# One-row tile first, and the first store set beside the third load: a row-gradient kernel that lives on its DMA queues

## The chip, the core and the metric

The kernel runs on one core of a Trainium2 chip. The metric is the device time of one execution in microseconds (us), taken as the median of several runs. Three executions of the kernel before took 1245.61, 1249.69 and 1249.73 us; the median is 1249.69 us.

## The reference

```python
def setup_inputs():
    return {"x": np.random.randn(8192, 8192).astype(np.float32)}

def reference(x):
    return np.gradient(x, axis=1)
```

Along each row of 8192 numbers, every inner element of the output is half the difference of its right and left neighbours. The first element is x[1] - x[0], the last x[8191] - x[8190]. Input and output are 268.44 MB each.

## The kernel before, in words

**Tiles.** The 8192 rows are cut into 21 groups of 384 rows and a rest of 128 rows. In a group each of the 128 partitions holds three whole rows one behind the other (`G = 3`), 24576 numbers. A group is loaded as two tiles of `W` = 12288 columns. The first tile of a group stores its first `CUT` = 12224 columns; the second stores the remaining 12352, for which it needs 64 columns from the end of the first (and one more to their left). The rest of 128 rows is one tile more, with one row of 8192 columns to a partition, and it comes last. That makes 43 tiles, numbered 0 to 42: 42 loads of 6144 KB and one of 4096 KB, 21 stores of 6112 KB, 21 of 6176 KB and one of 4096 KB.

**Slots.** Four buffers (`NB = 4`) take turns: tile i lives in slot i mod 4. A result is written into the same slot, 64 columns further left (`SH`), so load and store of a tile use one buffer. Load i+4 therefore has to wait until store i has landed.

**Queues.** All loads are issued by SyncE (SP, line 60) on one hardware DMA queue (q1 in the profile), all stores by ScalarE (ACT, line 127) on another (q10). Both queues are served by the same 16 DMA engines. A transfer has 128 partition rows, eight for each engine. The order in which instructions are issued is the order in which they are written (`manual_schedule`), and waits that a kept one implies are declared away in `chain`.

**Work on a tile.** When load i has landed, GpSimd (POOL) takes the one-sided differences at row ends and row starts into the small tile `ends` (line 83, two instructions). For the second tile of a group it also copies 65 columns from the slot of the first (line 90, the "halo"). VectorE (DVE) then runs one custom instruction over the tile (line 101, the difference times one half) and puts the saved row ends and starts in place with two small copies (line 124). Then ACT issues the store. For tile 0 alone there is an extra VectorE instruction (line 111): it reads 800 columns of the slot, writes them to a tile `spare` that nobody uses, and so holds the first store back.

The lines that set the order of the loads:

```python
        needed = [stores[i - NB]] if i >= NB else []        # L61
        ...
        for i in range(NB):                                  # four loads at the start
            load(i)
        ...
                if i - 1 + NB < nt:                          # behind a halo copy
                    load(i - 1 + NB)
        ...
            if (first or i == nt - 1) and i + NB < nt:       # behind a second tile's store
                load(i + NB)
```

Of the kernel before, what the change touches and what calls it, by code (L numbers as in the profile page):

```python
# [1 line left out]

# [4 lines left out]


@with_exitstack
def kernel(  # L10
    ctx: ExitStack,
    tc: tile.TileContext,
    x: bass.AP,
    out: bass.AP,
):
    nc = tc.nc
    P = nc.NUM_PARTITIONS
    n, m = x.shape
    NB = 4
    G = 3  # L20
    SH = 64
    IN = 2 * SH
    W = G * m // 2
    CUT = W - SH
    f32 = x.dtype

    tiles = []
    ngroups = n // (P * G)
    left = n - ngroups * P * G
    for g in range(ngroups):  # L30
        rows = slice(g * P * G, (g + 1) * P * G)
        xr = x[rows, :].rearrange("(p q) m -> p (q m)", p=P)
        orr = out[rows, :].rearrange("(p q) m -> p (q m)", p=P)
        tiles.append((xr[:, 0:W], orr[:, 0:CUT], 0, W, CUT))
        tiles.append((xr[:, W : 2 * W], orr[:, CUT : 2 * W], W, W, 2 * W))
    for r in range(n - left, n, P):
        tiles.append((x[r : r + P, :], out[r : r + P, :], 0, m, m))
    nt = len(tiles)

    pool = ctx.enter_context(tc.tile_pool(name="pool", bufs=1))  # L40
    pad = pool.tile([P, 32], f32, name="pad", tag="pad")
    slots = [pool.tile([P, IN + W], f32, name=f"slot{k}", tag=f"slot{k}") for k in range(NB)]
    ends = pool.tile([P, nt, 4], f32, name="ends", tag="ends")
    spare = pool.tile([P, 800], f32, name="spare", tag="spare")
    loads, stores, halos = [], [], {}
    in_front = {}

    def chain(i, ins, *needed):
        group, engine = f"slot{i % NB}", ins.ins.engine
        keep = [o.ins for o in needed]  # L50
        if in_front.get(engine, (None,))[0] == group:
            keep.append(in_front[engine][1])
        tc.declare_no_dep(ins.ins, group=group, keep=keep, reason="implied by the needed step")
        tc.add_to_no_dep_group(group, ins.ins)
        in_front[engine] = group, ins.ins
        return ins

    def load(i):
        src, _, _, w, _ = tiles[i]
        ins = nc.sync.dma_start(out=slots[i % NB][:, IN : IN + w], in_=src)  # L60
        needed = [stores[i - NB]] if i >= NB else []  # L61
        if i - NB + 1 in halos:
            needed.append(halos[i - NB + 1])
        loads.append(chain(i, ins, *needed))

    with tc.manual_schedule():
        for i in range(NB):
            load(i)
        for i in range(nt):
            b = slots[i % NB]  # L70
            _, dst, first, w, last = tiles[i]
            begin = CUT if first else 0
            at = lambda c: IN + c - first
            row = [c for c in range(0, G * m, m) if begin <= c < last]
            tail = [c for c in range(m - 1, G * m, m) if begin <= c < last]

            pieces = [(tail, -1, 0, 2), (row, 0, 1, 0)]
            taken = []
            for cols, lo, hi, e in pieces:
                k = len(cols)  # L80
                a = at(cols[0])
                z = a + (k - 1) * m + 1
                ins = nc.gpsimd.tensor_sub(  # L83
                    out=ends[:, i, e : e + k],
                    in0=b[:, a + hi : z + hi : m],
                    in1=b[:, a + lo : z + lo : m],
                )
                taken.append(chain(i, ins, loads[i]))
            if first:
                ins = nc.gpsimd.tensor_copy(  # L90
                    out=b[:, IN - SH - 1 : IN],
                    in_=slots[(i - 1) % NB][:, IN + W - SH - 1 : IN + W],
                )
                tc.declare_no_dep(ins.ins, group=f"slot{(i - 1) % NB}", keep=[], reason="implied by the subtractions in front")
                halos[i] = chain(i, ins, *taken)
                taken.append(halos[i])
                if i - 1 + NB < nt:
                    load(i - 1 + NB)
            a = at(begin) + (0 if first else 1)
            z = at(last) - (1 if last % m == 0 else 0)  # L100
            ins = nc.vector._custom_dve(  # L101
                dve_ops.TENSOR_TENSOR_REDUCE_SUB_MAX,
                out=b[:, a - SH : z - SH],
                in0=b[:, a + 1 : z + 1],
                in1=b[:, a - 1 : z - 1],
                s0=0.0,
                s1=0.5,
            )
            done = chain(i, ins, *taken)
            if i == 0:  # L110
                ins = nc.vector._custom_dve(  # L111
                    dve_ops.TENSOR_TENSOR_REDUCE_SUB_MAX,
                    out=spare[:, :],
                    in0=b[:, IN + W - 800 : IN + W],
                    in1=b[:, IN + W - 800 : IN + W],
                    s0=0.0,
                    s1=0.5,
                )
                done = chain(i, ins, done)
            for cols, lo, hi, e in pieces:  # L120
                k = len(cols)
                a = at(cols[0]) - SH
                z = a + (k - 1) * m + 1
                ins = nc.vector.tensor_copy(out=b[:, a:z:m], in_=ends[:, i, e : e + k])  # L124
                done = chain(i, ins, done)
            a = at(begin) - SH
            ins = nc.scalar.dma_start(out=dst, in_=b[:, a : a + last - begin])
            stores.append(chain(i, ins, done))
            if (first or i == nt - 1) and i + NB < nt:
                load(i + NB)  # L130


# [1 line left out]
_INS = ['x']  # L134
_OUTS = [((8192, 8192), 'float32')]


# [23 lines left out]
```

## Time and profile before

| | |
|---|---|
| median of 3 runs | 1249.69 us (1245.61 to 1249.73) |
| profiled execution | 1250.2 us, its span 1248.4 us |
| VectorE busy | 563.6 us, 45% of the span |
| GpSimd busy | 18.4 us, 1% |
| moved | 536.91 MB, mean 430 GB/s over the span |
| load of 6144 KB, issue to landing | median 50.8 us |
| store of 6176 KB / 6112 KB, issue to landing | median 51.4 / 51.6 us |

The span is the stretch that the profiler's records cover; the execution's own time is 1.8 us longer. The profile's table of 40 slices gives, for each fortieth of the span, the mean busy share of the 16 DMA engines (9 is 90% or more) and the GB/s that they moved. A packet is counted in the slice in which it starts. One data packet is one partition's row of a transfer, 48 KB for most loads.

### The profile page before, as it was taken

The numbers are of one execution on the slowest core, as the hardware profiler recorded it, in microseconds if no ns is written. First come the engines' busy times: TensorE is split into PE (matmuls) and PEld (weight loads), VectorE is DVE, ScalarE is ACT, GpSimd is POOL, SyncE is SP. The second block draws the span as 40 slices with busy tenths as digits, with TensorE's granted clock in tenths as the row PEclk, the third lists the DMA queues.
The fourth block names the chain that finished last, engine by engine and source line by source line (L and its number), as shares of the span: only waits on it lengthen the run. The fifth ranks groups of instructions, "written<-read, shape, count | busy, mean of one in ns | idle before, by whom it ended". The sixth has DMA issues, their size and how long they took to land.

```text
span 1248.4 us, 450 instructions
## 1 busy us (share of the span) xinstructions
DVE 563.6 (45%) x130; POOL 18.4 (1%) x111
## 2 busy tenths in 40 slices
DVE  4544444444444444444454444444444545444442
POOL 0000000000000000000000000000000000000000
DMA  9999999999999999999999999999999999999997
GB/s 403 426 429 427 439 442 430 428 429 447 433 429 428 434 443 431 429 429 442 438 430 429 431 442 435 430 429 442 436 432 429 431 440 436 432 427 438 438 431 329
DMA packets 12388, 536.91 MB, mean 430 GB/s; under 512 B 1376, under 2 KB 1376, under 8 KB 1376
## 3 DMA queue, kind: packets, MB, share of 16 engines
q1 hardware_dynamic: 6192, 268.44, 49.9%
q10 hardware_dynamic: 6192, 268.44, 49.7%
q14 instruction: 4, 0.03, 0.0%
HBM read 268.44 MB, written 268.44 MB: 430 GB/s over the span
## 4 chain that ended last, share of the span: by engine, by line
another core or an unknown queue 92%; DMA 3%; issue 2%; POOL 1%; DVE 1%; SPq 0%; POOLq 0%; DVEq 0%
DMA slot<-in_x_dram 3%; POOL ends L83 1%; DVE slot L101 1%; POOL slot L90 0%; SPq L60 0%; POOLq L156 0%; DVE slot L124 0%; DVEq L156 0%
## 5 line engine op out<-in xcount | busy, mean ns | idle before, releaser
L101 DVE CUSTOM_DVE_ANT_0 slot<-slot 128x12223 f32<-128x12223 f32 (+2 forms) x43 | 552.9, 12859 | 663.9 <-POOL ends L83 340.8
L83 POOL TENSOR_TENSOR ends<-slot 128x1 f32<-128x1 f32 (+1 forms) x86 | 14.5, 193 | 1201.4 <-DMA slot<-in_x_dram 1201.4
L124 DVE COPY slot<-ends 128x1 f32<-128x1 f32 (+1 forms) x86 | 9.7, 157 | 1.4
L90 POOL COPY slot<-slot 128x65 f32<-128x65 f32 x21 | 5.0, 238 | 0.0
L111 DVE CUSTOM_DVE_ANT_0 spare<-slot 128x800 f32<-128x800 f32 x1 | 1.0, 992 | 0.0
L145 POOL MEMSET const-float32-0.0<- 128x1 f32 x1 | 0.1, 98 | 0.2 <-issue 0.2
L145 POOL MEMSET const-bfloat16-1.0<- 128x1 bf16 x1 | 0.1, 101 | 0.0
L145 POOL MEMSET const-uint8-127<- 128x1 uint8 x1 | 0.1, 101 | 0.0
L145 POOL MEMSET const-float32-1.0<- 128x1 f32 x1 | 0.1, 98 | 0.0
## 6 DMA issues: line engine op xcount, KB each, us to landing
slot<-in_x_dram SPq DMA_DIRECT2D x42, 6144.0 KB, 50.8
out_dram<-slot ACTq DMA_DIRECT2D x21, 6176.0 KB, 51.4
out_dram<-slot ACTq DMA_DIRECT2D x21, 6112.0 KB, 51.6
slot<-in_x_dram SPq DMA_DIRECT2D x1, 4096.0 KB, 45.9
out_dram<-slot ACTq DMA_DIRECT2D x1, 4096.0 KB, 18.4
```

What stands on the lines that cost most here:

```text
L83: ins = nc.gpsimd.tensor_sub(out=ends[:, i, e : e + k], in0=b[:, a + hi : z + hi : m], in1=b[:, a + lo : z + lo : m],)
L90: ins = nc.gpsimd.tensor_copy(out=b[:, IN - SH - 1 : IN], in_=slots[(i - 1) % NB][:, IN + W - SH - 1 : IN + W],)
L101: ins = nc.vector._custom_dve(dve_ops.TENSOR_TENSOR_REDUCE_SUB_MAX, out=b[:, a - SH : z - SH], in0=b[:, a + 1 : z + 1], in1=b[:, a - 1 : z ...
L111: ins = nc.vector._custom_dve(dve_ops.TENSOR_TENSOR_REDUCE_SUB_MAX, out=spare[:, :], in0=b[:, IN + W - 800 : IN + W], in1=b[:, IN + W - 80 ...
L124: ins = nc.vector.tensor_copy(out=b[:, a:z:m], in_=ends[:, i, e : e + k])
L145: nc = _bacc.Bacc("TRN2", target_bir_lowering=False, num_devices=1)
```

## The change

The rest of 128 rows becomes tile 0 instead of tile 42, and the groups follow as tiles 1 to 42, starting at row 128. The extra VectorE instruction of tile 0 covers 1400 columns instead of 800, from the slot's start. The last tile is now the second half of a group; its VectorE work is cut at a row's start (column 16384) into two pieces of 4160 and 8192 output columns, each followed by its own small copies and its own store. The condition that decides where a load is issued in the program follows the new numbering.

```diff
+    SPARE = 1400
...
-    ngroups = n // (P * G)
-    left = n - ngroups * P * G
-    for g in range(ngroups):
-        rows = slice(g * P * G, (g + 1) * P * G)
+    left = n % (P * G)
+    for r in range(0, left, P):
+        tiles.append((x[r : r + P, :], out[r : r + P, :], 0, m, m))
+    singles = len(tiles)
+    for r in range(left, n, P * G):
+        rows = slice(r, r + P * G)
...
-    for r in range(n - left, n, P):
-        tiles.append((x[r : r + P, :], out[r : r + P, :], 0, m, m))
...
-    spare = pool.tile([P, 800], f32, name="spare", tag="spare")
+    spare = pool.tile([P, SPARE], f32, name="spare", tag="spare")
...
-            a = at(begin) + (0 if first else 1)
-            z = at(last) - (1 if last % m == 0 else 0)
...
+            cuts = [begin, last]
+            if i == nt - 1:
+                cuts[1:1] = [c for c in row if c > begin]
+            done = None
+            for lo, hi in zip(cuts, cuts[1:]):
+                a = at(lo) + (1 if lo % m == 0 else 0)
+                z = at(hi) - (1 if hi % m == 0 else 0)
                 ins = nc.vector._custom_dve(
                     dve_ops.TENSOR_TENSOR_REDUCE_SUB_MAX,
-                    out=spare[:, :],
-                    in0=b[:, IN + W - 800 : IN + W],
-                    in1=b[:, IN + W - 800 : IN + W],
+                    out=b[:, a - SH : z - SH],
+                    in0=b[:, a + 1 : z + 1],
+                    in1=b[:, a - 1 : z - 1],
...
+                done = chain(i, ins, *taken, *([done] if done else []))
+                if i == 0:
+                    ins = nc.vector._custom_dve(
+                        dve_ops.TENSOR_TENSOR_REDUCE_SUB_MAX,
+                        out=spare[:, :],
+                        in0=b[:, IN : IN + SPARE],
+                        in1=b[:, IN : IN + SPARE],
...
+                for cols, e in ((tail, 2), (row, 0)):
+                    inside = [k for k, c in enumerate(cols) if lo <= c < hi]
+                    if inside:
...
+                        ins = nc.vector.tensor_copy(out=b[:, a:z:m], in_=ends[:, i, e : e + k])
+                        done = chain(i, ins, done)
+                a = at(lo) - SH
+                ins = nc.scalar.dma_start(out=dst[:, lo - begin : hi - begin], in_=b[:, a : a + hi - lo])
+                stored = chain(i, ins, done)
+            stores.append(stored)
-            if (first or i == nt - 1) and i + NB < nt:
+            if (first or i < singles) and i + NB < nt:
                 load(i + NB)
```

## The prediction

> **What bounds the kernel now.** I read the page's parts 1 to 3 first: is any engine full?
>
> ```profile
> DVE 563.6 (45%) x130; POOL 18.4 (1%) x111
> DMA  9999999999999999999999999999999999999997
> GB/s 403 426 429 427 439 442 430 428 429 447 433 429 428 434 443 431 429 429 442 438 430 429 431 442 435 430 429 442 436 432 429 431 440 436 432 427 438 438 431 329
> q1 hardware_dynamic: 6192, 268.44, 49.9%
> q10 hardware_dynamic: 6192, 268.44, 49.7%
> ```
>
> The DMA engines are full in every slice but the last, half by loads (q1), half by stores (q10). VectorE is idle more than half the time. The windows view puts numbers on the stages (columns: stretch and its length, DVE and POOL busy, clock, DMA share, GB/s):
>
> ```profile
> 100.00:600.00 500.00, 226.85 (x54) 7.14 (x42) 1.00 1.00 433
> 600.00:1200.00 600.00, 267.63 (x61) 9.01 (x53) 1.00 1.00 434
> 1236.00:1242.00 6.00, 0.00 (x0) 0.00 (x0) 1.00 0.84 360
> 1242.00:1248.40 6.40, 0.00 (x0) 0.00 (x0) 1.00 0.05 20
> ```
>
> At 433.5 GB/s the 536.9 MB take 1238.5 us, so only about 10 of the span's 1248.4 us can be anything but bytes. Where are they? The DMA view of 28 to 48 us, in slices of 0.5 us, shows packets starting together on all engines:
>
> ```profile
> GB/s 492 98 0 1376 98 98 492 983 98 0 1278 197 98 0 1475 0 98 0 0 0 1369 98 98 295 1180 0 98 1271 196 0 196 1376 0 98 782 685 0 98 1376 98
> ```
>
> The crests stand 3 or 4 slices apart, one packet (48 KB at 433.5/16 GB/s = 1.81 us), but between 35.0 and 38.0 us there are 6: the load packet ahead of the first store's took 3.0 us, 1.2 more, on all engines. The same view of 1242 us to the end, in slices of 0.16 us:
>
> ```profile
> DMA  0400000004000000400000004000000000000000
> GB/s 0 205 0 0 0 0 0 0 0 205 0 0 0 0 0 0 205 0 0 0 0 0 0 0 205 0 0 0 0 0 0 0 0 0 0 0 0 0 0 0
> ```
>
> Four lone packets, 1.2 us apart (32 KB each): one DMA engine still works and fifteen are done. In the trace's landing records the last store lands on the first engine at 1241.35 us, on the fifteenth at 1243.24, on the last at 1247.47: this engine is 4.2 us behind. Following its 688 packets back, each to the one that ended where it began, I find it 1.2 us long at the first load packet, 1.6 at the first store, and then 4.75 us in 27 stretched packets, nearly all loads beside a boundary between two stores (0.34 at 90 us, 0.85 at 148, 0.73 at 389) and rare after 560 us, when it trails the others. The 10 us are: 1.7 to the first packet, 0.7 in it, 1.2 at the first store, 4.2 of the last engine, about 1.3 behind its last packet, and under 1 unassigned.
>
> **The change, part by part.**
>
> *Tile order.* The same 43 loads and 43 tiles, the same bytes: 0. Packets cost their bytes: 48 KB took 1.815 us and 32 KB 1.213 us.
>
> *The first store's place.* These rows give the times:
>
> ```profile
> 18.68 12.89 DVE L101 CUSTOM_DVE_ANT_0 slot<-slot 128x12223 f32<-128x12223 f32 x1 [18.68 <-POOL ends L83]
> 31.61 0.99 DVE L111 CUSTOM_DVE_ANT_0 spare<-slot 128x800 f32<-128x800 f32 x1
> 32.77 70.41 ACTq L127 DMA_DIRECT2D out_dram<-slot  x4
> 1220.05 8.69 DVE L101 CUSTOM_DVE_ANT_0 slot<-slot 128x8190 f32<-128x8190 f32 x1 [10.69 <-POOL ends L83]
> ```
>
> 8190 against 12223 elements give 1.042 ns per element and 0.16 us fixed (800 would be 0.99, as measured); 1400 make 1.62 us. Load 0 is 8 x 0.602 = 4.8 us shorter, so VectorE starts at 13.9, ends its pass at 22.6, the extra one at 24.2, the copies at 24.4, where ACT issues store 0. Before, the issue came 1.35 us after load 2's first packet (31.42), and load packets two and three went ahead of the store. Now, 4.8 us earlier than in the packet records of before (29.6 and 31.4), load 1's eighth packet starts at 24.8 and load 2's first at 26.6; issued 0.36 us ahead of the eighth (0.46 before), the store follows load 2's first packet, at about 29.6. So packet k of store j runs beside packet k of load j+2. The extra 0.63 us of VectorE costs nothing: loads 1 to 3 keep the engines full until 81. Without that cover it would cost 0.63. The 1.2 us at a first store I leave in: nothing here takes it away (bounds 0 and -1.2).
>
> *Slots.* Load 4 waits for store 0, which lands at about 53.7 us, and its turn comes when load 3 ends, at 81: 27 us ahead (22 before: issued at 66.9, first packet at 88.8). Load 5 and the rest stand behind it in SP's queue, with their own stores to wait for, and the halo copies they need are over 50 us old. No starving: 0. Median issue to landing should rise for loads from 50.8 to about 57, and fall for stores from 51.5 to about 44 (13.6 us after landing they are issued, and two periods of 29 us after it they end).
>
> *The last tile.* One VectorE pass becomes two (4159 elements, 4.49 us; 8190, 8.69 us) with a third copy (0.15 us), and one store becomes two. Count from T, where the last engine ends its final load packet. One more store packet (1.8) and the landing (0.4) precede POOL and VectorE (0.6); the first piece is issued at T+7.5, the second at T+16.5. That engine has store packets until T+16.3 (1.8 + 8 x 1.81) and, with the first piece (8 x 0.614), until T+21.2. From issue to first packet it took 1.0 us at the first load and 5.3 at the first store, which queued behind three packets; by the worse the second piece is 0.6 late, by the better 3.7 early. I take 0, by the row of an empty queue. The engines that are ahead may stand still 2 to 4 us; they are not last. The 128 more packets are 8 on each engine: 1.213 and 1.815 us leave 9 ns fixed in a packet, so 0.07 us.
>
> *The boundaries.* Now both queues change tile at once on every engine, 41 times. Before, each change has the other queue's data beside it. Rows near it: load 0 to load 1 alone, no gap; store 40 to store 41 alone, 0.06 us at most; the first store, 1.2. I take 0, since the two rows for a change between full transfers are nearest, and keep 1.2 for the range of the rival below.
>
> *The last engine.* Its 4.2 us cannot fall below 0, and can grow; its stretches sat at store boundaries, which now move onto load boundaries. I take no change.
>
> Sum: 1250.2 + 0.07 = 1250.3 for a profiled execution; the profiled one stands 0.5 above the median, so **1249.8 us**. Its own range is 1247 to 1253.
>
> 0.5% is 6.2 us (1243.4 and 1255.9), about what a measurement of this kernel can tell from no change. The largest gain in sight is 4.2 + 1.2 = 5.4 us.
>
> [...]
>
> **The rivals.**
>
> *The last engine catches up.* With both boundaries together no load packet lies between a store's last packet and its landing, and the 4.75 us of stretches could vanish: 1249.7 - 4.2 = 1245.5; with the first store's 1.2 us too, 1244.3. For it: the stretches' place, and 1245.61 us among the runs. Against it: the same engine was late at the start without any boundary.
>
> *Joint boundaries cost time on all engines.* Two landings and two first packets follow one another with no data between. If every engine then loses what the late one lost at 90 us, 41 x 0.34 = 14 us: 1264. It decides from 6.2/41 = 0.15 us a boundary; by the first store's 1.2 us it would be 49 us. Against it: the two lone boundaries at 0 and 0.06.
> [...]
>
> *The store misses its place* by one packet (0.4 us of issue time decide): pairs don't form, offsets as before, 1249.8.
>
> *The last piece is late*: 0.6 us, 1250.4.
>
> **How the numbers follow.** Forecast 0.50; last engine catches up 0.25, of which 0.06 past 0.5% if the start improves too and the measurement adds a little; joint boundaries 0.18, of which 0.16 past 0.5%; place missed 0.04; last piece late 0.03. Faster 0.06, same 0.50 + 0.19 + 0.02 + 0.07 = 0.78, slower 0.16. The range 1243.5 to 1258 leaves out the 0.06 below and, of joint boundaries, what costs over 0.2 us each (0.14): 0.2 together.
>
> **What would show it.** Right: store 0 issued near 24.4 us and starting at 29.6; landing medians near 57 and 44; middle windows at 433 to 434 GB/s; a share near 0.06 in the last few us. The rival of joint boundaries shows as middle windows under 431 GB/s; the late engine's recovery as a DMA share that falls from 0.9 to 0 within 2 us. Wrong altogether: DMA share under 0.98 in the middle, or a stretch without packets ahead of the last store.

## The result and the profile after

The changed kernel took 1446.47 us (median of 6 runs, 1443.80 to 1451.23) against 1249.71 us for the kernel before in the same comparison: a ratio of 1.159, 95% interval 1.156 to 1.162. I had forecast no change. The profiled execution took 1443.8 us, its span 1442.0 us, 193.6 us more than before.

The page of the changed kernel, the lines that answer to those shown of before:

```profile
DVE 564.4 (39%) x132; POOL 18.4 (1%) x111
DMA  9999999999999999999999999999999999999997
GB/s 400 397 379 376 370 366 376 375 368 369 373 369 374 371 373 375 372 374 369 375 366 372 374 372 369 370 372 370 372 371 371 372 370 373 371 371 369 376 376 338
q10 hardware_dynamic: 6336, 268.44, 50.1%
q1 hardware_dynamic: 6192, 268.44, 48.8%
```

VectorE and GpSimd do the same work in the same time. The DMA engines are as busy as before, 90% or more in all slices but the last, and move the same 536.91 MB. But from the third slice to the one before the last they move 366 to 379 GB/s where they moved 427 to 447. A row of nines says that the engines have a packet in hand, not that the packet moves at full speed: the loss is seen in the GB/s line alone. The windows of the changed kernel (stretch, its length, DVE, POOL, clock, DMA share, GB/s) say the same by stage:

```profile
4.00:32.00 28.00, 14.54 (x5) 0.67 (x4) 1.00 0.99 417
100.00:600.00 500.00, 189.83 (x46) 6.46 (x38) 1.00 0.99 372
600.00:1200.00 600.00, 233.83 (x54) 7.13 (x42) 1.00 1.00 371
```

The loss is even over the kernel: 371.5 against 433.5 GB/s. By these rates 536.9 MB take 1445 against 1238.5 us.

Which part of a tile is slow? The DMA view of 608 to 628 us, slices of 0.5 us, packets counted where they start, first of the kernel before, then of the changed one:

```profile
GB/s 99 99 1087 296 99 492 786 295 0 889 593 99 197 984 295 98 492 983 98 0 979 489 98 197 1081 295 0 782 685 98 98 1081 295 98 489 978 98 0 885 589
```

```profile
GB/s 392 294 392 392 393 393 98 588 392 196 294 391 491 294 294 491 587 196 196 587 294 491 196 393 686 294 98 783 197 393 295 294 589 490 98 393 490 295 393 295
```

Before, the engines start their packets together, a crest of 780 to 1090 GB/s in a slice, every 1.8 us. After, the crests are gone; engines start at any time. The trace's packet records (start, duration, bytes, queue) show why: a store packet that took 1.81 us now takes up to 2.6, a load packet up to 3.7. Of the packets 36% of the loads and 60% of the stores are stretched by over 0.1 us, against 1% and 0.02% before, and a load's eight packets are stretched alike (0.22 to 0.28 us on the mean), the store's too (0.27 to 0.31). So it is not something that happens once at a tile's boundary. Summed over an engine the stretches are 83.3 us in loads and 103.2 us in stores, against 2.6 and 0.2 before: 183.7 of the 193.6 us. By the same records 15.9 engines have a packet in hand on the mean from 100 to 1200 us, against 16.0 before; 0.1 of 16 over the kernel is about the 10 us that remain.

The start went as the change says. The timeline of the changed kernel:

```profile
13.44 8.69 DVE L106 CUSTOM_DVE_ANT_0 slot<-slot 128x8190 f32<-128x8190 f32 x1 [13.44 <-POOL ends L83]
22.16 1.62 DVE L116 CUSTOM_DVE_ANT_0 spare<-slot 128x1400 f32<-128x1400 f32 x1
23.93 17.49 ACTq L135 DMA_DIRECT2D out_dram<-slot  x2
```

Store 0 is issued at 23.93 us. By the packet records load 2's first packets start at 26.6 to 27.2 us and store 0's at 29.2 to 29.8, right behind them, on all 16 engines. Store 0 itself, with its 32 KB packets, still runs nearly at full speed (its fifth to eighth packets are up to 0.24 us longer, all its packets 0.03 us on the mean); from store 1's first packet at 53.4 us on every engine is slow. At the other end, when the loads are done, store 41 runs alone from about 1408 us on and its packets are back at 1.81 us.

### The profile page after: what moved, and what is told of

Its sections match the earlier page's. It is cut to its first block, busy times and chain, and to the rows that moved or that the text cites. A ratio compares the mean times of both kernels' runs of the same rounds, so it can differ in the third digit from the quotient of the medians.

```text
span 1442.0 us, 453 instructions
## 1 busy us (share of the span) xinstructions
DVE 564.4 (39%) x132; POOL 18.4 (1%) x111
## 2 busy tenths in 40 slices
DMA packets 12532, 536.91 MB, mean 372 GB/s; under 512 B 1392, under 2 KB 1392, under 8 KB 1392
## 4 chain that ended last, share of the span: by engine, by line
another core or an unknown queue 92%; issue 3%; DMA 2%; POOL 1%; DVE 1%; SPq 0%; POOLq 0%; DVEq 0%
DMA slot<-in_x_dram 2%; POOL ends L83 1%; DVE slot L106 1%; POOL slot L90 0%; SPq L61 0%; DVE slot L132 0%; POOLq L165 0%; DVEq L165 0%
## 5 line engine op out<-in xcount | busy, mean ns | idle before, releaser
L106 DVE CUSTOM_DVE_ANT_0 slot<-slot 128x12223 f32<-128x12223 f32 (+3 forms) x44 | 553.1, 12570 | 860.3 <-POOL slot L90 434.6
```

The source lines that it names most:

```text
L106: ins = nc.vector._custom_dve(dve_ops.TENSOR_TENSOR_REDUCE_SUB_MAX, out=b[:, a - SH : z - SH], in0=b[:, a + 1 : z + 1], in1=b[:, a - 1 : z ...
```

## The experiments

Names used below. Theory P: the place of the store's packets against the load's is what slows. Theory O: the tile order (one-row tile first, groups from row 128) is. If P holds, why? A: on an engine, HBM addresses of load and store fall together. B: on an engine, a load packet and the store packet beside it touch the same partition of two slots. J: transfers of both queues end together. Which partition an engine's packet holds the records do not show: that an engine takes the same eight neighbouring partitions, in order, from both queues is an assumption of mine, and what the expectations say of partitions and rows that meet rests on it. "Place 0" is that of the changed kernel: packet k of a store right behind packet k of the load two tiles later; "+1" is one load packet later.

Each run but the timed one near the end is a single execution; six executions of the kernel before lie between 1245.61 and 1251.27 us, so a few us between single runs say nothing.

**Place or order? Four kernels.** In the kernel before, the first store is moved to place 0:

```diff
             z = at(last) - (1 if last % m == 0 else 0)
+            if i == 0:
+                z = a + 9740
...
-            if i == 0:
-                ins = nc.vector._custom_dve(     # the extra pass goes
```

> The kernel before with its one-row tile last, but with the first store moved up to stand beside load 2's first packet: tile 0's VectorE pass covers 9740 of its 12223 columns (the rest of tile 0 is left uncomputed) and the extra pass is gone, so store 0 is issued near 29.3 us instead of 32.8. Theory P (the place: packet k of a store beside packet k of the load two tiles later is what slows every packet): about 1445 us, middle windows at 372 GB/s. Theory O (the order: the one-row tile first, with the groups from row 128 on, is what slows it): about 1250 us, 433 GB/s.

In the changed kernel the first store is moved to later places by more extra passes (2 of 1495 columns, 3 of 1525, 5 of 1552):

```diff
-    SPARE = 1400
+    SPARE = 1495
+    PASSES = 2
...
-                if i == 0:
+                for _ in range(PASSES if i == 0 else 0):
```

> The changed kernel with a second extra pass, so that the first store comes one load packet later (beside load 2's second packet). Theory P with packets on equal rows at fault: fast again, 1250 to 1255 us and 433 GB/s. Theory P with the tiles' joint ends at fault: the ends are one packet apart, partly better, 1250 to 1400. Theory O: 1445 us.

> The changed kernel with three extra passes: the first store two load packets later, beside load 2's third, where the kernel before has it. Theory P: about 1250 us, 433 GB/s. Theory O: 1445 us, 372 GB/s.

> The changed kernel with five extra passes: the first store four load packets later. Theory P: 1250 us. Theory O: 1445 us. A value between (1300 to 1400) would speak for a conflict that depends on how far apart the rows are that a load and a store touch at one time.

Measured: the kernel before in place 0, 1436.71 us; the changed kernel at +1, +2 and +4: 1253.46, 1245.61 and 1253.15 us (the kernel before beside them 1249.66). The windows of the kernel before in place 0:

```profile
100.00:600.00 500.00, 197.82 (x45) 6.46 (x38) 1.00 0.97 382
600.00:1200.00 600.00, 237.31 (x54) 7.64 (x45) 1.00 0.96 376
```

and of the changed kernel at +2:

```profile
100.00:600.00 500.00, 224.20 (x51) 7.33 (x43) 1.00 1.00 434
600.00:1200.00 600.00, 276.80 (x63) 8.86 (x52) 1.00 1.00 434
```

Theory P holds and theory O falls: the old order is slow in place 0, the new order is fast out of it. In the first of these kernels store 0's first packets come at 34.2 us or later, on ten engines behind load 2's first packet and on six (from 36.5 us) behind its second. The packet records show stretched packets from 41.5 us on (stores up to 2.46 us, loads up to 3.2), while load 2 and store 0, the first tiles to end near each other, end after 59 us. Joint ends therefore can't have begun it: theory J in its plain form falls.

The same records show that a stretched store packet goes with the place of its own engine. The first ones, from 41.51 to 42.65 us, are the third store packets of the ten engines in place 0, 0.28 to 0.65 us longer; on the six other engines no store packet is stretched by then. From 60 to 1200 us, of the packets whose place the records tell, a store packet in place 0 is 0.22 us longer on the mean, one in any other place less than 0.01 us; load packets are longer in all places, 0.28 us ahead of a store in place 0 and 0.09 to 0.14 elsewhere. Here the stretches sum to 125 us for an engine, and the DMA share of 0.96 to 0.97 leaves some 50 us without a packet.

One load packet more or less decides 190 us. At +1 there is a small loss (432 and 430 GB/s in the windows; 9.5 us of stretched loads to an engine), at +2 and +4 none (434 GB/s in both windows of each).

**One packet earlier.** The extra pass goes, and tile 0's pass covers 7790 of 8190 columns.

```diff
+                if i == 0:
+                    z = a + 7790
...
-                if i == 0:
-                    ins = nc.vector._custom_dve(     # the extra pass goes
```

> The changed kernel without any extra pass and with tile 0's VectorE pass over 7790 of its 8190 columns (the rest of tile 0 is left uncomputed), so that the first store is issued near 21.9 us and comes one load packet earlier than in the changed kernel, right behind load 1's last packet. Then packet k of a store runs just ahead of load packet k instead of just behind it, and tiles of both queues still end side by side. Theory B (the same partition beside each other on an engine) and theory J: slow, 1400 to 1450. If only a store packet right behind the load packet of its own place is slow: fast, 1245 to 1255.

Measured: 1245.78 us, and the windows are those of a fast kernel:

```profile
100.00:600.00 500.00, 224.21 (x51) 7.36 (x43) 1.00 1.00 434
600.00:1200.00 600.00, 276.45 (x61) 8.89 (x52) 1.00 1.00 434
```

The packet records show that the place was not quite the one that I had aimed at. Load 1's landing took a turn of its queue, so two store packets followed each other (as in the kernel before, where from 60 to 1200 us at least 608 of the 624 records of a load's landing, 9 ns each, lie between two store packets), and from then on store packet k+1 stands ahead of load packet k: the store leads by between one and two packets. No store packet lies beside the load packet of its own number here, so this run does not decide on theory B. It does bound the slow place on the early side.

**HBM addresses (theory A).** Every group tile of the changed kernel is loaded from some rows further up than it is stored; nothing else moves:

```diff
-        xr = x[rows, :].rearrange("(p q) m -> p (q m)", p=P)
+        xr = x[r - 3 : r - 3 + P * G, :].rearrange("(p q) m -> p (q m)", p=P)
```

> The changed kernel, pairs in time as they are, but every group tile is loaded from 3 rows (one partition's share, 96 KB of HBM) further up than the rows it stores, so the results are of shifted rows. Only the HBM addresses of the loads move; partitions in the slots, queues, waits and joint ends stay. Theory A (a load and a store on an engine touch HBM addresses that fall together): 1245 to 1255 us, packets back at 1.81. Theory B (both touch the same partition of the slots): still 1445. Theory J (tiles of both queues end together): still 1445.

> As the run with 3 rows, with 128 rows (4 MB of HBM) instead. Theory A in the form that addresses fall together when they agree up to some power of two of at most 4 MB: slow again, 1430 to 1450. Theory A in the form that only one certain distance between load and store matters: fast, 1250. Theories B and J: 1445, as with 3 rows, so this run tells something only if that one is fast.

> The changed kernel with every group tile loaded from 24 rows (8 partitions' share, 768 KB of HBM) further up than the rows it stores. With 3 rows a store's packet still lay beside the next load packet of the same rows; with 24 no packet of that engine beside it does. Theory A (HBM addresses of a load and a store on one engine fall together): fast, 1245 to 1255 us. Theory B (same partition of the slots on one engine): slow, 1440 to 1450.

And the converse, at +2, with 6 rows:

> The converse: the kernel with the first store two load packets later (1245.6 us), with every group tile loaded from 6 rows further up, so that in time the store's packets k = 1, 2, 5 and 6 meet load packets k + 2 of the same addresses relative to their tile; half of all packets meet, none of the tile ends do. Theory A: clearly slower, about half of the loss, 1300 to 1400 us. Theories B and J: 1245 to 1255, as without the shift.

Measured: 1442.17 us with 3 rows, 1446.42 with 128, 1443.06 with 24; the converse 1249.63. The windows with 24 rows:

```profile
100.00:600.00 500.00, 186.75 (x46) 6.46 (x38) 1.00 0.99 372
600.00:1200.00 600.00, 237.28 (x54) 7.13 (x42) 1.00 0.99 371
```

Theory A falls for the distances tried. The distance in HBM between what an engine reads and writes at one time can be changed by 96 KB, 768 KB or 4 MB without changing the time (the run with 4 MB could have told something only by being fast), and addresses that, by the assumed order, meet at +2 do no harm. (By the same order, with 3 rows a store's packet still met the next load packet's rows; the run with 24 closes that gap.)

**Halves of 64 partitions: four runs that told nothing of it.** Loads and stores of the changed kernel were cut into two DMAs of 64 partitions, in equal or opposite order. The line that issues a load also stands elsewhere in the program, with SyncE's order of loads as it was. The part for the loads:

```diff
...
+        for h in LH:
+            half = slice(64 * h, 64 * h + 64)
+            ins = nc.sync.dma_start(out=slots[i % NB][half, IN : IN + w], in_=src[half, :])
...
```

> The changed kernel with every load and store (but the last tile's stores) cut into two DMAs of 64 partitions, lower half first in both, pairs in time as in the changed kernel. On an engine a load packet and the store packet beside it still touch the same partition of two slots, and the DMAs end together. Theory B (same partition): slow, 1400 to 1450. Theory J (DMAs of both queues end together): slow, or slower still since there are twice as many joint ends.

> As before it, but loads take the upper half of the partitions first and stores the lower half. The DMAs end together as there, but load and store beside each other on an engine touch partitions 64 apart. Theory B: fast, 1245 to 1255, 433 GB/s. Theory J: slow, 1400 or more.

> Halves in the same order, with the first store four load packets later (five extra passes). A store's lower half runs beside a load's upper half: no partition met, tiles end apart, but the half DMAs of both queues still end together. Theory B: fast, 1245 to 1255. Theory J for every DMA: slow. Theory J for whole tiles alone: fast.

> Halves in opposite order, with the first store four load packets later. Now a store's lower half runs beside the load's lower half: partitions meet on every engine, while tiles end half a tile apart. Theory B: slow, 1400 to 1450. Theory J for every DMA: slow. Theory J for whole tiles alone: fast, 1245 to 1255. Together the four runs tell these apart: B is slow, fast, fast, slow; J for every DMA is slow in all four; J for tiles is slow, slow, fast, fast.

Measured: 1651.61, 1656.25, 1662.05 and 1641.32 us. All slow, as theory J for every DMA would have it, but the windows of the first show a reason that has nothing to do with places. The last line is of the run with 24 rows, for comparison:

```profile
4.00:24.00 20.00, 0.00 (x0) 0.12 (x1) 1.00 1.07 223
100.00:600.00 500.00, 169.54 (x39) 5.12 (x30) 1.00 1.00 334
4.00:24.00 20.00, 10.43 (x4) 0.34 (x2) 1.00 1.01 436
```

From 4 to 24 us there are loads alone, and they already run at 223 GB/s where loads of 128 partitions ran at 436 in the same stretch of the run with 24 rows. Why, the runs do not show, nor how the 334 GB/s of the mixed stretch come about. These four runs are no test of B or J.

**Pieces of 24 KB, with all 128 partitions.** Each partition row of a load and a store is moved as two pieces (loads read 64 columns twice, stores leave 64 or 128 out). The part for the loads; in the second run a load is two DMAs of half the columns instead:

```diff
...
+        h = w // 2
+        two = bass.AP(src.tensor, src.offset, [list(src.ap[0]), [h - 64, 2], [1, h]])
+        ins = nc.sync.dma_start(out=slots[i % NB][:, IN : IN + w].rearrange("p (t h) -> p t h", t=2), in_=two)
...
```

> The changed kernel with every partition row of a load and a store moved as two pieces of about 24 KB, so that an engine's 16 packets of a tile go by partitions 1,1,2,2,...,8,8 in both queues. Loads read 64 columns twice and stores leave 64 or 128 columns out, so the results are not the reference's. The extra pass covers 830 columns, for a first store beside load 2's first packets (within a packet). Theory B: slow, over 1350, since a load packet and the store packet beside it touch one partition.

> The run with row pieces, but each load is two DMAs of half the columns, so that an engine's load packets go by partitions 1,2,...,8,1,2,...,8 while the store's go 1,1,2,2,...,8,8. Tiles of both queues still end together, packets have the same size, the same engine moves the same partition; only 3 of 16 packets beside each other share a partition. Theory B: fast or nearly so, 1245 to 1290. Theory J (tiles that end together): as slow as with row pieces.

> The run with row pieces and three extra passes of 1350 columns, so that the first store comes 3.5 us, four packets of 24 KB, later: two partitions apart. It shows whether pieces cost anything by themselves. Theory B: fast, 1245 to 1260. If it is slow, pieces are slow by themselves and the other two tell nothing.

> The run with row pieces, with the extra pass lengthened from 830 to 1455 columns (0.65 us), so that the first store follows load 2's first piece instead of coming ahead of it: piece j of a store then runs exactly between pieces j and j+1 of a load, in the place of the changed kernel. Theory B, or any theory in which equal places of the two queues are what slows: slow, 1350 to 1450 us. If it is fast (1245 to 1255), the same partition on an engine is not the cause, and the slow place exists only for packets of one 48 KB row.

Measured: 1248.17, 1267.09, 1244.68 and 1250.44 us. Pieces cost nothing by themselves (433 GB/s in both windows of the third). (The second run, with two DMAs to a load, moves 431 and 429 GB/s in its windows; I did not follow the rest of its 17 us.) But the first was to be slow, and so was the last. By the packet records the first missed the place: on 14 engines two store pieces went ahead of load 2's first piece. The last, with 0.65 us more of VectorE, hit it on half of the engines: on eight the store followed load 2's first piece, on eight its second. It stayed so. In place 0 both queues end a tile together on an engine, and the landing of a store is written within 0.03 us behind that of a load; from 60 to 1200 us this holds for all store landings of the changed kernel, for none at +1, and for 51% in the last run with pieces. The windows of the last show at most a trace of loss:

```profile
100.00:600.00 500.00, 224.22 (x51) 7.36 (x43) 1.00 1.00 431
600.00:1200.00 600.00, 273.90 (x61) 8.89 (x52) 1.00 1.00 432
```

So place 0 with 24 KB pieces is not slow on eight engines. From 60 to 1200 us a store piece there is 0.007 us longer on the mean and the load piece ahead of it 0.0004 us, against 0.33 and 0.25 us for the packets of the changed kernel in the same stretch; in the kernel before in place 0, ten engines had been enough for 190 us. Every store piece in place 0 follows the load piece of its own number. If both queues take the pieces in the same order of partitions, as I assumed and the records, which have no partitions, do not show, the two touch the same partition. So this run speaks against B, and for the length of the packet, 48 KB against 24, as a condition of the slowness. A run with all 16 engines in place 0 is missing.

**The fast place, timed.** The changed kernel at +2, twelve executions beside seventeen of the kernel before.

> The changed kernel with the first store two load packets later, timed. All theories: 1243 to 1250 us, the same as the kernel before or up to 0.4% faster, if the last DMA engine falls behind less.

Measured: ratio to the kernel before 1.0009, 95% interval 0.9997 to 1.0022. (The medians, 1249.27 and 1246.27 us, lie further apart, since each kernel's times fall into two groups, of which more below.) No version here beats the kernel before by anything that shows.

All places of the store with 48 KB packets and 128 partitions, with the mean GB/s of the stretch 600 to 1200 us:

| first store against load 2's packets | order of tiles | us | GB/s |
|---|---|---|---|
| leads by one to two packets | one-row tile first | 1245.78 | 434 |
| place 0 (the change) | one-row tile first | 1446.47 | 371 |
| place 0 on ten engines, +1 on six | one-row tile last | 1436.71 | 376 |
| +1 | one-row tile first | 1253.46 | 430 |
| +2 | one-row tile first | 1249.27 | 434 |
| +2 (the kernel before) | one-row tile last | 1249.71 | 434 |
| +4 | one-row tile first | 1253.15 | 434 |

The 3.9 us from +2 to +4 are not the place but the last engine's delay, told below.

## Why the prediction was wrong, point by point

**Right: the change's own mechanics.** I had VectorE at 13.9, the issue at 24.4 and the first store packet at 29.6 us, behind load 2's first packet; they came at 13.4, 23.9 and 29.2, in that place. The extra pass took 1.62 us, as worked out. The rival that the store misses its place did not happen.

**Wrong: the step on the boundaries, and the sum that it rests on.** I asked what two boundaries at one time cost, took 0 from load 0 to load 1 and from store 40 to store 41, and let all other packets cost "their bytes". The term that failed is the duration of a packet, which I had as fixed at 1.815 us and which holds for a load or a store alone and, but for 0.03 us on the loads at +1, for both out of place 0. In place 0 it is on the mean 0.24 us longer for a load packet and 0.29 for a store packet. The rows I chose could not have shown it: in none of them did packets of equal number run side by side, and I carried the rate of one place over to another. I had worked out that packet k of store j would run beside packet k of load j+2, and then priced only what happens between tiles.

**The rival on the slower side** had the direction and nearly the right circumstance, "both queues change tile at once on every engine", with the wrong mechanism. It put the loss at the 41 boundaries (14 us, at most 49) where it sits on every packet (183.7 us), and in the kernel before in place 0 packets were slow before any two tiles had ended together. My sign for it, middle windows under 431 GB/s, came true for another reason, so it could not tell the two apart; my sign for being wrong altogether, a DMA share under 0.98, did not come (0.99 and 1.00 in the windows), since slow packets keep an engine busy.

**Landings.** I expected medians of about 57 us for loads and 44 for stores. The page after:

```profile
slot<-in_x_dram SPq DMA_DIRECT2D x42, 6144.0 KB, 67.7
out_dram<-slot ACTq DMA_DIRECT2D x21, 6112.0 KB, 54.5
out_dram<-slot ACTq DMA_DIRECT2D x20, 6176.0 KB, 54.2
```

They were two periods of 29 us less what lies ahead of the issue; a period is now 34 us (two transfers of 6.29 MB at 371 GB/s), which adds 10 to each, and that is what was added. The mechanics of the queue held, the period did not.

**The last engine.** I left its 4.2 us in and gave its recovery 0.25. At +2 (1245.61 us) and one packet early (1245.78 us) its last landing is 0.03 us and 0.02 us behind the fifteenth's, against 4.2 us in the profile of before; at +4 (1253.15 us) it is 7.7 behind. The timed runs fall into two groups, near 1246 and near 1249.5, for the kernel before as for +2; the profiled one of +2 with 1248.8 us has a last engine 3.7 us behind. So this term explains the scatter in the profiled executions, but whether an execution has it did not follow from the place in the runs seen.

**The last tile.** I took 0 and let engines that are ahead stand still for 2 to 4 us. In the changed kernel the DMA share is 0.95 from 1400 to 1410 us, 0.85 to 1430 and 0.87 to 1438, in sum 4.5 us of an engine's time on the mean, and the last store's landings spread over 4 us; what of this the end waited for is not known. At +2, with the same last tile, the fifteenth engine's last landing came at 1242.91 us, against 1243.24 in the kernel before, so there the last tile cost nothing that shows.

**The bound on what could happen.** My range rested on bounds for what could be saved and on boundary prices for what could be lost. I had no bound on the rate itself, though the whole time is that rate. A change that alters which packets meet deserved one.

**Still open** is what it is in place 0. Shown: the place and not the order; not the HBM distances tried; not begun by joint ends; stores are stretched on the engines that are in place 0. Two things the runs speak on without showing them: against the same partition, and for the length of the packet, since 24 KB pieces in place 0 on eight engines cost next to nothing and store 0, with its 32 KB packets, ran nearly at full speed. What two queues share at an engine when equal packets of 48 KB follow each other, the runs do not say.

## What to carry to other kernels

In a kernel that lives on two DMA queues, the phase of one queue against the other is a parameter of its own: scan it in steps of one packet, by delaying the first store, before trusting a tidy alignment, and leave a margin of two packets to a slow place, since 0.65 us of VectorE moved the store by two to three packets of 24 KB. Moving a row in two pieces may take the slow place away; on eight engines it did. Read the GB/s line beside the busy line: engines that are busy throughout can still have lost 14% of their rate. And when a change alters which transfers run side by side, price each packet and not only the boundaries.

## What the runs showed of the hardware

- Two queues, each with packets of 48 KB, shared 16 engines at 430 to 434 GB/s in most places and at 371 in one, with the same bytes, addresses and partitions.
- In that place a store packet of 48 KB was 0.33 us longer and a piece of 24 KB, on eight engines, 0.007 us. Where ten of 16 engines began in it, the first stretched stores were on these ten alone.
- In the kernel before, the engines but for the late one start packets within about 1 us of each other; in place 0 at any time. Loading and storing at one time is not by itself slow: at +1, from 700 to 1000 us, eight engines load and eight store for a third of the time, at 430 GB/s.
- A landing takes a turn of its queue: behind a load's last packet the records show two store packets in a row, with the 9 ns record of the landing between them (at least 608 of 624 times in the kernel before, from 60 to 1200 us). So one step of delay does not always move the store by one packet, and the place between "leads by one to two packets" and place 0 was not reached.
- Loads of 64 partitions ran at 223 GB/s, of 128 at 436.
